# A mixer layer on one core: the first two row blocks modulated as a pair, x first in the queue, and even chunks

## The chip, the cores and the metric

The kernel runs on one core of a Trainium2 chip. The metric is the device time of one execution in microseconds, as the median of several runs. The engines are TensorE (PE; its weight loads are PEld), VectorE (DVE), ScalarE (ACT), GpSimd (POOL) and SyncE (SP, here only a queue that issues transfers).

## The reference

One layer of a decoder trunk on x of 512 x 2048, in float32:

```python
cond = jax.nn.silu(c)
mod = cond @ w_ada[l] + b_ada[l]
shift, scale, gate = jnp.split(mod, 3, axis=-1)
h = rms_norm(x, norm_g[l]) * (1.0 + scale[:, None, :]) + shift[:, None, :]
z = h @ w_in[l]
u_a, v_a, g_a, q_b, k_b, v_b, g_b, f_b = jnp.split(z, pts, axis=-1)
...
y = jnp.concatenate([y_a, y_b], axis=-1) @ w_out[l]
x = x + gate[:, None, :] * y
return rms_norm(x, final_g)
```

`y_a` is a chunked gated MLP of u, v and a gate, `y_b` is attention over 16 heads with a forget gate, times a gate. `c` is one vector of 2048, `w_ada` is 2048 x 6144 (shift, scale, gate), `w_in` 2048 x 7184, `w_out` 2048 x 2048.

## The kernel before

All big products are made of float32 operands cut into a high and a low part: three matmuls (high x high, high x low, low x high) for one. x and h are held transposed, as 16 row blocks of 128 model columns by 512 positions. A block k of h is made by `make_h` out of the transposed, normalised x (`xT[k]`) with a shift `sh` and a scale `gs` of one column each: `hh[k]` is its high, `hl[k]` its low part.

Shift and scale come from a product of one vector with w_ada. `ada_step(q, i)` loads a piece of w_ada (shift and scale columns of group q, some row blocks), and VectorE multiplies each row block by its element of silu(c), held as columns in `sc`, and adds it to an accumulator. `make_h(q)` then sums the accumulator over the partitions with matmuls of one column against `ones` (tile `mod`), adds the biases (L272 to L274) and makes hh and hl. The table `ADA` lists the groups: blocks 0 and 1 alone (pieces of 128 columns, four row blocks a load), all others in pairs (256 columns, two row blocks a load). Accumulators of the pairs and `mod` share the single PSUM bank with the tag "c".

At the start c, norm_g, b_ada and two small vectors are loaded to `rows` and turned into columns by TensorE; then x comes in four tiles of 128 positions, all on SP's queue. ScalarE squares each x tile (L311), the reciprocal root is taken (L91), VectorE scales the tile (L313), TensorE transposes it in pieces (L321) and ScalarE copies them out of PSUM (L325). Between these stand 32 matmuls on w_ada pieces that compute nothing that is used (`warm`, L208).

Then the first stage ("stream", tiles named `s` and `st`) multiplies 14 column groups of w_in (u and most of the gate of group A) with h, in chunks of row blocks listed in `CH`: six chunks of two and one of four. The 14 groups are in two sets, which share the same seven PSUM banks ("mm" four, "b" three): within a chunk one set runs, its partial sums are put aside or added (`sp`, L407 and L410), then the other set, which goes on in the next chunk. Each weight tile is loaded (`raw_st`), its high part made by ScalarE (L127) and its low part by VectorE or GpSimd (L128). During chunk q the steps of `ADA` for the blocks of chunk q+1 are put between the weight tiles; as many as fit into the tiles but one. `load` chains the transfers of SP's queue in the order of the program until the second chunk.

After the stream come value, query, key and gate groups of attention (`v_group`, `qk_group`, `g_group`), each with its banks from "mm"; a list of `fillers`, one taken after each weight tile, loads the gate columns of w_ada, which GpSimd sums, and `gate_sum` adds them over the partitions with a matmul. Attention slots, the rest of group A and the output projection follow. Instructions are ordered on each engine at build time by a planner that goes by priorities (`tc.high_priority`, `tc.issue_after`) and its own estimate of times.

Of the kernel before, what the change touches and what calls it, by code (L numbers as in the profile page):

```python
# [27 lines left out]
def trunk_kernel(  # L28
# [66 lines left out]
    CHAIN = [1]  # L95

# [59 lines left out]
    def col_group(segs, evs, name):  # L156
        nb = sum(w for _, w in segs) // P
        banks = [bank("mm", f"{name}_{b}") for b in range(nb)]
# [13 lines left out]
    rows = st.tile([80, P], F32, name="rows")  # L172
    nc.sync.dma_start(rows[0:16, :], c[0].rearrange("(a b) -> a b", b=P))
    nc.sync.dma_start(rows[16:32, :], norm_g[0].rearrange("(a b) -> a b", b=P))
    nc.sync.dma_start(rows[32:64, :], b_ada[0, 0 : 2 * D].rearrange("(a b) -> a b", b=P))
    nc.sync.dma_start(rows[64:72, :], ln_g[0].rearrange("(a b) -> a b", b=P))
    nc.sync.dma_start(rows[72:80, :], ln_b[0].rearrange("(a b) -> a b", b=P))

# [6 lines left out]
    cols_p = bank("c", "cols_p")  # L185
    nc.tensor.transpose(cols_p[:, 0:80], rows, ident[0:80, 0:80])
    cols = const.tile([P, 80], F32, name="cols")
    nc.vector.tensor_copy(cols, cols_p[:, 0:80])
# [13 lines left out]
    SPL = (0, 1)  # L202
    WARM = 4
    wbank = bank("c", "warm")

    def warm(src, n):
        for i in range(n):
            nc.tensor.matmul(wbank[:, 0:128], ident, src, start=True, stop=True)  # L208

    ADA = [(0, 1), (1, 1), (2, 2), (4, 2), (6, 2), (8, 2), (10, 2), (12, 2), (14, 2)]  # L210
    LANE = "DEDE"

    def ada_step(q, i):
        k0, nk = ADA[q]
        w = nk * P
        per = 4 // nk
        ga = st.tile([P, per, 2, w], F32, name=f"ada{q}_{i}", tag="ada", bufs=8)
        for s in range(2):
            load(
                ga[:, :, s, :], ada_r[:, i * per : (i + 1) * per, s, k0 * P : k0 * P + w]  # L220
            )
        if q == 0:
            warm(ga[:, 0, 1, :], WARM)
        if q in SPL:
            if i == 0:
                three = st.tile([P, 2, 256], F32, name=f"acca{q}", tag="acc", bufs=2)
                accs[q] = {
                    "D": three[:, 0, :].rearrange("p (s n) -> p s n", s=2),
                    "E": three[:, 1, :].rearrange("p (s n) -> p s n", s=2),
                }  # L230
            for j in range(per):
                kk = i * per + j
                ln = LANE[j]
                a = accs[q][ln]
                eng = nc.vector
                if i == 0 and ln not in LANE[:j]:
                    eng.tensor_scalar(a, ga[:, j], sc[:, kk : kk + 1], None, ALU.mult)
                else:
                    eng.scalar_tensor_tensor(a, ga[:, j], sc[:, kk : kk + 1], a, ALU.mult, ALU.add)
            return  # L240
        if i == 0:
            accs[q] = (
                bank("c", f"acc{q}"), st.tile([P, 2, 256], F32, name=f"accs{q}", tag="acc", bufs=2)
            )
        pt = accs[q][0]
        a = pt[:, 0 : 2 * w].rearrange("p (s n) -> p s n", s=2)
        sb = accs[q][1][:, :, 0:w]
        for j in range(per):
            kk = i * per + j
            if kk == 0:  # L250
# [633 lines left out]
```

## Time and profile before

| | us |
|---|---|
| median of 3 runs | 934.62 (934.34 to 935.93) |
| profiled execution | 936.01 |
| its span, first to last instruction | 934.3 |
| TensorE busy in it | 899.5 |

Times in the rows are microseconds from the start of the span. A row of a timeline gives the start, the duration, engine, line, operation, output and inputs with their shape, the count of instructions merged into it, and in square brackets the idle time of the engine ahead of it with what ended that. Shapes are partitions x elements. A window row gives for each engine the busy time and instructions in that stretch, then TensorE's granted clock as a share of 2.4 GHz, the busy share of the transfer engines and what they moved in GB/s.

### The profile page before, as it was taken

The page shows a single profiled execution, that of the slowest core. Times are in us where ns is not written, and L with a number is a line of the kernel's source. Part 1 is how long each engine was busy: PE and PEld are TensorE (multiplying, and loading weights), DVE is VectorE, ACT ScalarE, POOL GpSimd, SP SyncE. Part 2 cuts the span into 40 slices and gives each one's busy share as a digit, 9 for nine tenths or more (in the row PEclk, how much of TensorE's full clock was granted, in tenths as well). Part 3 has the DMA queues.
Part 4 walks back from the last instruction along what each step waited for, and adds up shares of the span by engine and source line. Part 5 has one row for each costly group of instructions (what it writes and reads, how often), then busy time and mean ns, then how long its engine had stood idle before and what let it go on. Part 6 is the DMA issues. An engine that isn't in the chain of part 4 may idle for free.

```text
span 934.3 us, 12387 instructions
## 1 busy us (share of the span) xinstructions
PE 899.5 (96%) x4485; PEld 764.7 (82%) x4485; DVE 537.0 (57%) x906; ACT 412.0 (44%) x724; POOL 325.5 (35%) x234
## 2 busy tenths in 40 slices
PE   4889989999999999999999999999999999999996
PEld 3768878889888887998889888998888888888884
DVE  4777776654545468456737664456424893445522
ACT  4634332353446446556436644556423532333311
POOL 1135553534002697897889910000000230000000
PEclk9999989999999999999999999999999999999999
DMA  8999997225333455435455443223233333446122
GB/s 297 333 356 351 305 300 231 80 61 140 100 92 113 120 171 152 158 117 168 143 163 180 148 114 99 82 70 91 77 103 90 102 106 116 151 143 226 61 111 91
DMA packets 117918, 142.75 MB, mean 153 GB/s; under 512 B 8400, under 2 KB 89504, under 8 KB 117344
## 3 DMA queue, kind: packets, MB, share of 16 engines
q1 hardware_dynamic: 117568, 141.43, 48.5%
q8 instruction: 35, 0.57, 0.3%
q10 hardware_dynamic: 288, 0.52, 0.2%
q14 instruction: 27, 0.22, 0.1%
HBM read 137.54 MB, written 4.19 MB: 152 GB/s over the span
## 4 chain that ended last, share of the span: by engine, by line
PE 86%; issue 2%; DMA 1%; DVE 1%; ACT 1%; POOL 1%; SPq 0%; POOLq 0%; ACTq 0%; DVEq 0%
PE s L143 5%; PE s L145 5%; PE s L144 5%; PE wo L154 5%; PE wo L153 5%; PE wo L152 5%; PE vb L153 3%; PE vb L154 3%; PE vb L152 3%; PE va L153 3%; PE k L143 3%; PE va L154 3%; PE va L152 3%; PE k L144 3%; PE k L145 3%; PE gb L144 3%
## 5 line engine op out<-in xcount | busy, mean ns | idle before, releaser
L603 POOL TENSOR_SCALAR gate<-gate,sc 128x512 f32<-128x512 f32 x60 | 108.6, 1818 | 21.5 <-DMA gate<-in_w_ada_dram 20.0
L143 PE MATMUL s<-hh,whi_st 128*128 128x512 f32 x224 | 87.5, 408 | 6.8 <-ACT hh L278 6.7
L128 POOL TENSOR_TENSOR wlo_st<-raw_st,whi_st 128x1024 fp32r<-128x1024 f32 (+3 forms) x32 | 63.8, 1999 | 82.8 <-ACT whi_st L127 81.3
L144 PE MATMUL s<-hl,whi_st 128*128 128x512 f32 x224 | 88.7, 396 | 2.3 <-POOL hl L289 2.3
L604 POOL TENSOR_TENSOR gate<-gate,gate 128x512 f32<-128x512 f32 x60 | 88.2, 1470 | 2.4
L145 PE MATMUL s<-hh,wlo_st 128*128 128x512 f32 x224 | 78.6, 396 | 0.0
L253 DVE SCALAR_TENSOR_TENSOR acc<-ada,sc,acc 128x512 f32<-128x512 f32 x98 | 74.0, 755 | 3.1
L152 PE MATMUL wo<-whi_wo,yh 128*128 128x512 f32 x192 | 74.8, 390 | 0.0
L153 PE MATMUL wo<-whi_wo,yl 128*128 128x512 f32 x192 | 74.7, 389 | 0.0
L153 PE MATMUL vb<-whi_vb,hl 128*128 128x256 f32 (+1 forms) x256 | 71.8, 286 | 0.0
L152 PE MATMUL vb<-whi_vb,hh 128*128 128x256 f32 (+1 forms) x256 | 71.8, 286 | 0.0
L154 PE MATMUL wo<-wlo_wo,yh 128*128 128x512 f32 x192 | 70.1, 390 | 0.0
L154 PE MATMUL vb<-wlo_vb,hh 128*128 128x256 f32 (+1 forms) x256 | 68.0, 285 | 0.0
L127 ACT ACTIVATE whi_st<-raw_st 128x1024 fp32r<-128x1024 f32 (+3 forms) x36 | 31.4, 873 | 80.5 <-PE s L144 44.4
L91 POOL TENSOR_TENSOR rsv<-rsv,nhalf 128x1 f32<-128x1 f32 x4 | 4.6, 1149 | 165.4 <-DVE rsv L90 165.4
L143 PEld LDWEIGHTS s<-hh,whi_st 128*128 128x128 f32 x224 | 43.5, 196 | 16.5 <-ACT hh L278 7.0
L849 POOL TENSOR_TENSOR sfin<-sfin,nhalf 128x1 f32<-128x1 f32 x4 | 2.2, 548 | 152.3 <-DVE sfin L846 152.3
L144 PEld LDWEIGHTS s<-hl,whi_st 128*128 128x128 f32 x224 | 42.9, 191 | 12.2 <-POOL hl L289 3.2
L143 PE MATMUL q<-hh,whi_q 128*128 128x512 f32 x128 | 50.4, 393 | 1.6 <-ACT ft L663 1.6
L143 PE MATMUL k<-hh,whi_k 128*128 128x512 f32 x128 | 50.4, 394 | 0.7 <-DVE q L455 0.7
L144 PE MATMUL gb<-hl,whi_gb 128*128 128x512 f32 x128 | 50.4, 394 | 0.0
L144 PE MATMUL q<-hl,whi_q 128*128 128x512 f32 x128 | 50.2, 393 | 0.0
(221 smaller groups left out, 2374.0 us busy)
## 6 DMA issues: line engine op xcount, KB each, us to landing
ada<-in_w_ada_dram SPq DMA_DIRECT2D x128, 256.0 KB
gate<-in_w_ada_dram SPq DMA_DIRECT2D x32, 512.0 KB
raw_wo<-in_w_out_dram SPq DMA_DIRECT2D x24, 512.0 KB
raw_q<-in_w_in_dram SPq DMA_DIRECT2D x16, 512.0 KB
raw_k<-in_w_in_dram SPq DMA_DIRECT2D x16, 512.0 KB
raw_gb<-in_w_in_dram SPq DMA_DIRECT2D x16, 512.0 KB
raw_va<-in_w_in_dram SPq DMA_DIRECT2D x16, 512.0 KB
raw_st<-in_w_in_dram SPq DMA_DIRECT2D x21, 384.0 KB
```

The costliest lines, as they stand in the source:

```text
L91: nc.gpsimd.tensor_tensor(dst, dst, nhalf[:, 0:1], ALU.pow)
L127: nc.scalar.activation(hi, raw, AF.Copy)
L128: (loeng or nc.vector).tensor_tensor(lo, raw, hi.bitcast(F32), ALU.subtract)
L143: nc.tensor.matmul(pt, hi[:, j, cs], hh[k], start=(k == first), stop=False)
L144: nc.tensor.matmul(pt, hi[:, j, cs], hl[k], start=False, stop=False)
L145: nc.tensor.matmul(pt, lo[:, j, cs], hh[k], start=False, stop=(k == last))
L152: nc.tensor.matmul(o, ah[k][:, tsl], hi[:, j, :], start=(k == first), stop=False)
L153: nc.tensor.matmul(o, al[k][:, tsl], hi[:, j, :], start=False, stop=False)
L154: nc.tensor.matmul(o, ah[k][:, tsl], lo[:, j, :], start=False, stop=(k == last))
L253: nc.vector.scalar_tensor_tensor(sb if kk == KB - 1 else a, ga[:, j], sc[:, kk : kk + 1], a, ALU.mult, ALU.add,)
L603: nc.gpsimd.tensor_scalar(ga[:, j], ga[:, j], sc[:, kk : kk + 1], None, ALU.mult)
L604: nc.gpsimd.tensor_tensor(a, a, ga[:, j], ALU.add)
```

## The change

Seven edits, most of them in the first stage.

- The small vectors are loaded on ScalarE's queue, c into a tile of its own; x is the first on SP's queue. c and the others are transposed apart, c into bank `cb`.
- 18 bf16 matmuls on a mask that is in SBUF from the start are put at TensorE's beginning (`BUSY`), and the 32 on w_ada pieces are dropped.
- `ADA` has pairs only: blocks 0 and 1 are modulated together, from eight steps of two row blocks with pieces of 256 columns. For this pair five of the 16 row blocks (`MV`) are multiplied on TensorE, as matmuls of one column into `cb`, to which the matmuls against `ones` then add.
- Block 0's h goes through a tile of its own on VectorE; block 1's hl is made by GpSimd as the others' are. The low part of the first weight tiles is made by GpSimd too.
- The x transposes 0 to 12 come ahead of the first `make_h`, and only the copies out of PSUM of 13 to 15 wait for its first activation; other banks are used for some.
- `CH` has eight chunks of two.
- The first query group takes its banks from the tags "b" and "c", and each `gate_sum` but the last comes three fillers later, the last after three empty ones.

```diff
-    rows = st.tile([80, P], F32, name="rows")
-    nc.sync.dma_start(rows[0:16, :], c[0].rearrange("(a b) -> a b", b=P))
...
+    crow = st.tile([16, P], F32, name="crow")
+    nc.scalar.dma_start(crow, c[0].rearrange("(a b) -> a b", b=P))
+    rows = st.tile([64, P], F32, name="rows")
+    for r0, nr, src in (
+        (16, 32, b_ada[0, 0 : 2 * D]), (0, 16, norm_g[0]), (48, 8, ln_g[0]), (56, 8, ln_b[0]),
+    ):
+        nc.scalar.dma_start(rows[r0 : r0 + nr, :], src.rearrange("(a b) -> a b", b=P))
...
+    cb = bank("c", "cb")
...
+    warm(cmask[:, 0:P], cmask[:, 0 : S - P], BUSY, True)
...
-    ADA = [(0, 1), (1, 1), (2, 2), (4, 2), (6, 2), (8, 2), (10, 2), (12, 2), (14, 2)]
-    LANE = "DEDE"
+    ADA = [(k, 2) for k in range(0, KB, 2)]
+    MV = (7, 9, 11, 13, 15)
...
+            if q == 0 and kk in MV:
+                for s in range(2):
+                    for n in range(2):
+                        newest_mm[0] = nc.tensor.matmul(
+                            cb[:, 2 * s + n : 2 * s + n + 1], ga[:, j, s, n * P : (n + 1) * P], col,
+                            start=(kk == MV[0] and s + n == 0), stop=False, skip_group_check=True,
+                        )
...
-            if q == 0:
+            h = xT[k]
+            if k == 0:
+                first_h[0] = z
+                h = st.tile([P, S], F32, name="h0", tag="acc", bufs=2)
                 nc.vector.tensor_scalar(
-                    xT[k], xT[k], gs[:, k : k + 1], sh[:, k : k + 1], ALU.mult, ALU.add
+                    h, xT[k], gs[:, k : k + 1], sh[:, k : k + 1], ALU.mult, ALU.add
                 )
...
-            (nc.vector if q == 0 else HL).tensor_tensor(hl[k], xT[k], hh[k].bitcast(F32), ALU.subtract)
+            (nc.vector if k == 0 else HL).tensor_tensor(hl[k], h, hh[k].bitcast(F32), ALU.subtract)
...
-    CH = [(0, 2), (2, 2), (4, 2), (6, 2), (8, 4), (12, 2), (14, 2)]
-    for i in range(4):
-        ada_step(0, i)
+    CH = [(0, 2), (2, 2), (4, 2), (6, 2), (8, 2), (10, 2), (12, 2), (14, 2)]
+    with tc.high_priority(offset=200):
+        for i in range(8):
+            ada_step(0, i)
...
-    HB = 8
+    HB = 12
...
-                        loeng=nc.gpsimd if gi in POOLG and (q or kk) else None,
+                        loeng=nc.gpsimd if gi in POOLG else None,
...
-                    if early:
-                        if gi:
-                            for f in early:
-                                f()
-                            early = []
+                    if q == 0 and kk == 0 and gi == 0:
                         continue
...
-        col_group([(Q0 + c0, 256)], [evac_q(2 * u), evac_q(2 * u + 1)], f"q{u}")
+        col_group([(Q0 + c0, 256)], [evac_q(2 * u), evac_q(2 * u + 1)], f"q{u}", "mm" if u else "x")
...
-                fillers.append(lambda g=g: gate_sum(g))
+                    if g and i == 2:
+                        fillers.append(lambda g=g: gate_sum(g - 1))
+            fillers.extend([lambda: None] * 3 + [lambda: gate_sum(3)])
```

## Rows read from the trace of the kernel before

**Rows 1.** The page's first part: busy time of each engine, its share of the span and its instructions.
```profile
PE 899.5 (96%) x4485; PEld 764.7 (82%) x4485; DVE 537.0 (57%) x906; ACT 412.0 (44%) x724; POOL 325.5 (35%) x234
```

**Rows 2.** Windows: from 240 us to the end, and the last of the windows of 20 us.
```profile
240.00:934.00 694.00, 684.57 (x3425) 581.87 (x3423) 380.69 (x642) 314.71 (x580) 228.93 (x153) 1.00 0.39 122
...
920.00:940.00 20.00, 5.27 (x24) 4.02 (x22) 2.69 (x5) 2.06 (x4) 0.55 (x1) 0.85 0.23 88
```

**Rows 3.** What TensorE's matmuls waited for over the whole span: us in total, times, longest.
```profile
PE s L143 <- ACT hh L278: 6.7, 3, 2.7
...
PE s L144 <- POOL hl L289: 2.3, 2, 2.0
PE q L143 <- ACT ft L663: 1.6, 1, 1.6
...
PE k L143 <- DVE q L455: 0.7, 1, 0.7
```

**Rows 4.** TensorE's timeline: transposes of x early and late in the ramp, the first matmul on hh, block 1, blocks 2 and 3, and the end of the stream.
```profile
11.98 1.75 PE L321 MATMUL xTp<-ident,x 128*128 128x128 f32 x7 [7.41 <-DVE x L313]
...
22.98 0.93 PE L321 MATMUL xTp<-ident,x 128*128 128x128 f32 x7
...
32.42 1.46 PE L143 MATMUL s<-hh,whi_st 128*128 128x512 f32 x5
...
37.59 0.72 PE L267 MATMUL mod<-ones,acca 128*128 128x1 f32 x6
39.82 1.91 PE L143 MATMUL s<-hh,whi_st 128*128 128x512 f32 x7 [1.51 <-ACT hh L278]
42.04 0.51 PE L144 MATMUL s<-hl,whi_st 128*128 128x512 f32 x1 [0.31 <-POOL hl L289]
...
58.30 1.88 PE L143 MATMUL s<-hh,whi_st 128*128 128x512 f32 x7 [2.47 <-ACT hh L278]
...
62.20 0.50 PE L144 MATMUL s<-hl,whi_st 128*128 128x512 f32 x1 [2.03 <-POOL hl L289]
...
207.53 0.28 PE L152 MATMUL vb<-whi_vb,hh 128*128 128x272 f32 x1
```

**Rows 5.** Groups of instructions by line and shape from 0 to 210 us: busy us, mean ns of one, idle time ahead of them. One of the stream's three kinds of matmul, the multiplies by silu(c), the added partial sums, and the low parts of weight tiles on GpSimd.
```profile
L143 PE MATMUL s<-hh,whi_st 128*128 128x512 f32 x224 | 87.5, 408 | 6.8 <-ACT hh L278 6.7
...
L253 DVE SCALAR_TENSOR_TENSOR acc<-ada,sc,acc 128x512 f32<-128x512 f32 x98 | 74.0, 755 | 3.1
...
L410 DVE TENSOR_TENSOR sp<-s,sp 128x512 f32<-128x512 f32 x42 | 28.3, 687 | 20.3 <-PE s L145 20.2
...
L128 POOL TENSOR_TENSOR wlo_st<-raw_st,whi_st 128x512 fp32r<-128x512 f32 x2 | 2.6, 1280 | 25.0 <-ACT whi_st L127 25.0
```

**Rows 6.** The chain that ended last, in order of time: start, us, what.
```profile
131.07 0.45 PE s L145 x2
...
132.21 0.80 PE mod L267 x8
...
135.71 0.79 PE s L143
```

**Rows 7.** Windows of 5 us with a granted clock under 1.00 (the value ahead of the transfer share).
```profile
60.00:65.00 5.00, 2.97 (x10) 2.25 (x10) 4.75 (x8) 0.36 (x1) 3.40 (x3) 0.83 1.08 361
65.00:70.00 5.00, 5.00 (x20) 4.06 (x19) 3.68 (x5) 0.63 (x2) 0.00 (x0) 0.83 1.09 354
...
135.00:140.00 5.00, 4.29 (x10) 3.38 (x11) 4.79 (x7) 2.77 (x4) 2.52 (x2) 0.50 0.85 262
140.00:145.00 5.00, 5.00 (x19) 4.00 (x19) 3.25 (x5) 0.00 (x0) 0.00 (x0) 0.82 0.96 322
```

**Rows 8.** Timelines of the ramp: SP's issues, ScalarE's pass over the last x tile, a weight pass and the copies, GpSimd's root and VectorE's scaling for the last x tile.
```profile
0.79 0.40 SPq L173 DMA_DIRECT2D rows<-in_c_dram  x1
...
2.89 2.08 SPq L104 DMA_DIRECT2D x<-in_x_dram  x4
...
15.27 1.91 ACT L311 ACTIVATE junk<-x 128x2048 bf16<-128x2048 f32 x1 [0.54 <-DMA x<-in_x_dram]
...
18.33 0.72 POOL L91 TENSOR_TENSOR rstd<-rstd,nhalf 128x1 f32<-128x1 f32 x1 [2.79 <-DVE rstd L90]
...
19.77 1.28 DVE L313 TENSOR_SCALAR x<-x,rstd 128x2048 f32<-128x2048 f32 x1
...
24.64 0.53 ACT L127 ACTIVATE whi_st<-raw_st 128x384 fp32r<-128x384 f32 x1
25.05 4.99 ACT L325 ACTIVATE xT<-xTp 128x512 f32<-128x512 f32 x10
```

**Rows 9.** Windows: while blocks 0 and 1 loaded w_ada, and two stretches in which pairs did. The last value is GB/s.
```profile
18.00:25.00 7.00, 7.00 (x47) 7.00 (x46) 6.67 (x16) 1.85 (x4) 0.72 (x1) 1.00 1.15 306
...
40.00:50.00 10.00, 9.69 (x42) 7.66 (x43) 9.26 (x14) 6.06 (x12) 2.59 (x2) 1.00 1.09 349
...
75.00:95.00 20.00, 20.00 (x93) 16.66 (x92) 17.37 (x28) 6.76 (x8) 12.16 (x7) 1.00 1.09 351
```

**Rows 10.** Timelines of GpSimd and VectorE around block 1: GpSimd's first low parts, and VectorE's wait for block 1's modulation and the first multiply for blocks 2 and 3.
```profile
37.64 2.23 POOL L128 TENSOR_TENSOR wlo_st<-raw_st,whi_st 128x512 fp32r<-128x512 f32 x2 [18.58 <-ACT whi_st L127]
...
38.35 0.16 DVE L272 TENSOR_TENSOR sh<-mod,cols 128x1 f32<-128x1 f32 x1 [4.49 <-PE mod L267]
...
38.84 0.74 DVE L251 TENSOR_SCALAR acc<-ada,sc 128x512 f32<-128x512 f32 x1
```

More of the change, by code (lines that the diff above doesn't have):

```diff
@@ L95, in trunk_kernel @@
     CHAIN = [1]
+    BUSY = 18
+    WARM = 0
     newest = [None]
@@ L154, in mm_toks, with col_group @@
                 nc.tensor.matmul(o, ah[k][:, tsl], lo[:, j, :], start=False, stop=(k == last))
-    def col_group(segs, evs, name):
+    def col_group(segs, evs, name, tag="mm"):
         nb = sum(w for _, w in segs) // P
-        banks = [bank("mm", f"{name}_{b}") for b in range(nb)]
+        banks = [bank(tag, f"{name}_{b}") for b in range(nb)]
         nk = 8 // nb
@@ L183, in trunk_kernel, with warm @@
         xt.append(xx)
-    cols_p = bank("c", "cols_p")
-    nc.tensor.transpose(cols_p[:, 0:80], rows, ident[0:80, 0:80])
-    cols = const.tile([P, 80], F32, name="cols")
-    nc.vector.tensor_copy(cols, cols_p[:, 0:80])
+    cb = bank("c", "cb")
+    def warm(lhs, rhs, n, first=False):
+        for i in range(n):
+            nc.tensor.matmul(
+                cb[:, P : P + rhs.shape[-1]], lhs, rhs, start=first, stop=True, skip_group_check=True
+            )
+    warm(cmask[:, 0:P], cmask[:, 0 : S - P], BUSY, True)
+    cols = const.tile([P, 80], F32, name="cols")
+    nc.tensor.transpose(cb[:, 16:32], crow, ident[0:16, 0:16])
+    nc.vector.tensor_copy(cols[:, 0:16], cb[:, 16:32])
+    cols_p = bank("b", "cols_p")
+    nc.tensor.transpose(cols_p[:, 0:64], rows, ident[0:64, 0:64])
+    nc.vector.tensor_copy(cols[:, 16:80], cols_p[:, 0:64])
     cT, ngT, bshT, bscT, lngb = (cols[:, 16 * i : 16 * (i + 1)] for i in range(5))
@@ L201, in trunk_kernel @@
     gate = gp_.tile([P, 4, 512], F32, name="gate")
[L202 to L208, printed above, removed]
-    ADA = [(0, 1), (1, 1), (2, 2), (4, 2), (6, 2), (8, 2), (10, 2), (12, 2), (14, 2)]
-    LANE = "DEDE"
+    ADA = [(k, 2) for k in range(0, KB, 2)]
+    MV = (7, 9, 11, 13, 15)
     def ada_step(q, i):
[L214 to L217, printed above, removed]
+        k0 = ADA[q][0]
+        ga = st.tile([P, 2, 2, 256], F32, name=f"ada{q}_{i}", tag="ada", bufs=8)
@@ L218, in ada_step @@
         for s in range(2):
-            load(
-                ga[:, :, s, :], ada_r[:, i * per : (i + 1) * per, s, k0 * P : k0 * P + w]
-            )
-        if q == 0:
[L223 to L240, printed above, removed]
@@ L241, in ada_step @@
-        if i == 0:
[L242 to L250, printed above, removed]
-                nc.vector.tensor_scalar(a, ga[:, j], sc[:, kk : kk + 1], None, ALU.mult)
+            load(ga[:, :, s, :], ada_r[:, 2 * i : 2 * i + 2, s, k0 * P : k0 * P + 256])
@@ new lines, in ada_step @@
+        if i == 0:
+            sb = st.tile([P, 2, 256], F32, name=f"accs{q}", tag="acc", bufs=2)
+            a = bank("c", f"acc{q}").rearrange("p (s n) -> p s n", s=2) if q else sb
+            accs[q] = (a, sb)
+        a, sb = accs[q]
+        for j in range(2):
+            kk = 2 * i + j
+            col = sc[:, kk : kk + 1]
+            if q == 0 and kk in MV:
[4 more added lines that the diff above has]
+                            start=(kk == MV[0] and s + n == 0), stop=False, skip_group_check=True,
+                        )
+            elif kk == 0:
+                nc.vector.tensor_scalar(a, ga[:, j], col, None, ALU.mult)
@@ L264, in make_h @@
         for s in range(2):
             for j in range(nk):
-                for n, part in enumerate(parts):
-                    newest_mm[0] = nc.tensor.matmul(
-                        mp[:, s * nk + j : s * nk + j + 1], part[:, s, j * P : (j + 1) * P],
-                        ones[:, 0:1], start=(n == 0), stop=(n == len(parts) - 1),
-                    )
+                newest_mm[0] = nc.tensor.matmul(
+                    mp[:, s * nk + j : s * nk + j + 1], accs[q][1][:, s, j * P : (j + 1) * P],
+                    ones[:, 0:1], start=q > 0, stop=True, skip_group_check=True,
+                )
@@ L369, in trunk_kernel @@
         ]
-        early = [f for z, (ka, _) in enumerate(ADA) if q == 0 and 0 < ka < sum(CH[0]) for f in ada_steps(z)]
         order = [0, 1] if (q + NQ) % 2 else [1, 0]
```

32 lines of the change are left out of this document (14 added, 18 removed).

## The prediction

> **What bounds the kernel now.** I read the profile from the whole to the place. The page's first part has TensorE at 96% of the span [rows 1]. The windows say where the rest is: from 240 us on it is idle for 9.4 us of 694, and 8.7 of these lie in the tail after 920 [rows 2]. So the change can only pay ahead of 240 us, where TensorE's waits and the granted clock tell what for. The waits name four causes behind the ramp: hh from ScalarE 6.7 us, hl from GpSimd 2.3, one wait of the first query group 1.6, and later one of 0.7 [rows 3].
>
> The first stretch is a ramp, then a stream. The stream begins with the first matmul on hh, at 32.42, and ends where the first value-group matmul starts, at 207.53 [rows 4]: 175.1 us. Its own work is 224 matmuls of each of three kinds (16 blocks x 14 column groups), 672 in all [rows 5]; two of them take 0.45 us in the chain, so one takes 0.2265 and all of them 152.2 us [rows 6]. Eight modulation matmuls take 0.80 [rows 6]; seven pairs of row blocks make 5.6 us, and block 1 some 1.0 us. The remainder is 175.1 - 152.2 - 6.6 = **16.3 us lost**. TensorE's timeline shows where [rows 4]: 1.51 us before block 1's hh and 0.31 before its hl; 2.47 and 2.03 us before blocks 2 and 3; and 2.7 us between the modulation of blocks 10 and 11 (132.21 + 0.80) and the matmul at 135.71 [rows 6]: 9.0 in all. The clock adds to it: in 60 to 70 us two windows of 5 us with mean 0.83 make 3.4 us at half rate (1.2 instead of 2.4 GHz), in 135 to 145 there are 6.8 us, 6.4 of them with work [rows 7]. Half of it is lost: 1.7 + 3.2 us. That leaves 2.4 us of restarts and small change.
>
> **The change part by part.**
>
> *x first.* SP issues five small loads from 0.79 us and x only at 2.89 [rows 8]; they go to ScalarE's queue, where five issues of 0.4 us end near 3 us, before the first x can have landed. x lands 2.1 us sooner: the last tile, which ScalarE starts at 15.27 [rows 8], at about 13.2.
>
> *Blocks 0 and 1 as a pair.* Both blocks' w_ada columns (16 loads of 256 KB, 4.19 MB) must now be there before the first matmul; before it was half. Against that the pieces grow from 512 B to 1 KB a row. With the short pieces the queue moved 306 GB/s, with the pairs' long ones 349 to 351 [rows 9]. 4.19 MB / 0.350 = 12.0 us, so the last lands at 13.2 + 12.0 = 25.2. The first two weight tiles (0.46 MB) follow by 26.5. VectorE multiplies 11 of 16 blocks instead of 16, each 0.755 us [rows 5], in all 8.3 us, and follows the loads: from tile 3 on it has one block per 1.5 us. TensorE takes the other five, 20 matmuls of one column; the nearest rows are six modulation matmuls in 0.72 us [rows 4], so 2.4 us, or 5 at half rate, among loads that they wait for anyway. After the last load: 0.3 us to start, 0.75 for VectorE, 0.5 for four modulation matmuls, and 1.5 from these to the matmul on hh (38.31 to 39.82 before [rows 4]). **Earliest start: 28.3.**
>
> The other chain is x. From ScalarE's last pass over x at 15.27 to the end of its scaling (19.77 + 1.28) it was 5.8 us [rows 8], so now about 19.0; then 13 copies out of PSUM at 0.5 us (ten in 4.99) and two weight passes of 0.6 [rows 8]: 26.7, just inside. If five of these copies stand behind the last load on ScalarE, or TensorE does the last 24 transposes after it, the start goes to 31 or 32. I take **29.3**, nearer to the lower end because both chains end there, 3.1 us before 32.42. The first lo parts move to GpSimd (1.28 us each [rows 5]): GpSimd had been idle for 18.6 us there [rows 10], it is needed only by the third matmul on, and costs nothing unless hl of block 1 queues behind it.
>
> *No wait at block 1.* Its 1.8 us go, and so does the delay that followed from it: VectorE sat 4.49 us until block 1's modulation matmuls, queued behind block 0's on TensorE, had run, and started on blocks 2 and 3 only at 38.84 [rows 10]. Now it starts at about 27.5. What is late next is w_ada of blocks 2 and 3: 4.19 MB plus 1.4 of the chunk's 1.84 MB of weights at 350 GB/s end at 25.2 + 16 = 41.2, VectorE at 42, and they are due when six of eight weight tiles are done, 29.3 + 14.3 = 43.6. The margin is small, so I keep one wait for hl as it stood there, 2.03 us, and its absence as the other end.
>
> *Chunks of two only.* A chunk takes 19.0 + 0.8 = 19.8 us of TensorE; it needs 6.03 MB, 17.2 us of transfers. VectorE has 16 x 0.755 and 7 partial sums added at 0.687 us [rows 5], 16.9 us. The one chunk of four had to prepare two pairs during the 20 us ahead of it; that is the stall at 133 us with its 6.8 us of slow clock. It goes: 2.7 + 3.2 = 5.9 us. The price is one more round of seven partial sums, 4.8 us of VectorE; the cover is the 2.9 us that VectorE has left in a chunk, and a stretch with just this load exists: 75 to 95 us, VectorE 17.4 and TensorE 20.0 of 20 us [rows 9].
>
> *First query group on other banks.* It waited 1.6 us for copies of the value group out of its banks [rows 3]. Value 1.6, other end 0 if the other banks or the weights are not ready either; the key group comes 21 us later and finds its banks free.
>
> *The gate sums* are put three steps later. No wait of TensorE for them is in rows 3; 0, and plus or minus 1 for the shifted turns of the banks. The 32 warming matmuls on w_ada fall away and 18 early ones come, in time in which TensorE has nothing else.
>
> **Sum.** Stream: 29.3 + 152.2 + 5.6 + lost time. Lost: 1.0 of restarts, 2.0 at block 2, 1.7 for one stretch of 3.4 us at half clock, since TensorE waits about 1.5 us ahead of the first matmul; 4.7 in all, with ends 0.5 and 8.5. End 191.8 against 207.5: 15.7, with the 1.6 of the query group **17.3 us**. The profiled execution took 936.01 us (span 934.3, and 1.7 around it that I leave); it would be 918.7. It lies 1.4 over the median of the runs, 934.62, which becomes **917.3**. Best case 28.3 and 0.5: 20.9 + 1.6 = 22.5, 912.1. Worst case 32 and 8.5: 9.2 + 0, 925.4.
>
> **The rivals.** *Cold start (0.17).* Seven transposes took 1.75 us at 11.98 and 0.93 at 22.98, after most of the warming matmuls on w_ada [rows 4]. So TensorE ran slowly in the gaps of the ramp and fast after steady work, though the granted clock reads 1.00 in both. The change has warming only in the first 8 us, ahead of those gaps. Then the 24 last transposes and the matvecs run at the slow rate and the stream starts at 31 with 6.8 us at half clock instead of 3.4: 1.7 + 1.7 us less gain, 920.7. The Trainium skill, "TensorE: Matmul & The Clock Gate", section on the clock gate, says that the low clock is the default and only sustained work lifts it; by that rule this speaks against the change, and the two rows of transposes agree with it. Against the rival: between 19 and 27 us transposes and matvecs themselves fill TensorE.
>
> *The start gains nothing (0.21).* In-order queues put x's scaling or the copies behind w_ada: start 32.4, block 2 keeps its waits and its clock (2.47 + 2.03 + 1.7) beside 2.3 of restarts. End 198.7, gain 8.8 + 1.6 = 10.4: 924.2. For it: x's last scaling already waited behind w_ada multiplies (its factor was ready at 19.05, it ran at 19.77 [rows 8]). Against it: x lands 2.1 us earlier and no warming matmul stands ahead of its transposes.
>
> *Slower (0.05): VectorE sets the pace of each chunk.* The multiplies of a pair start only after the pair before has been modulated, since both use one PSUM bank (38.84, right behind block 1's [rows 10]). 16.9 us of VectorE and 1.5 until hh are 18.4 of 19.8 us. If a chunk misses that, it pays as at 133 us, 5.9 us; three such chunks eat the gain, seven would give 917.3 + 41 = 958. Against it: 75 to 95 us.
>
> That the chunks do not even out, the stall at 133 staying while the rest works, I give 0.03: 917.3 + 5.9 = 923.2.
>
> **How the numbers follow.** The forecast has 0.54. Its own range, 912.1 to 922, and the rivals at 920.7, 923.2 and 924.2 lie within **912.5 to 925.0**, which leaves out the slower case and the two thin ends. A measurement here tells 0.2%, 1.9 us, from no change. Faster 0.94 (all but the slower rival and a little); the same 0.02; slower 0.04, as one or two such stalls would still leave it faster.
>
> **What would show it.** In the changed kernel: x passes on ScalarE from about 5.7; the last w_ada near 25; first hh matmul at 28.3 to 30; no gap at block 1; the first value-group matmul at 188 to 196; clock 1.00 from 45 to 240; no wait ahead of the first query group. Wrong: a start after 32, half clock in more than one stretch of the stream, or waits for hh at the chunk borders.

## The result, and the profile after

The changed kernel takes **921.17 us** (919.59 to 922.33), the kernel before in the same rounds 934.95 (934.34 to 935.93), four runs each: ratio 0.9851, with a 95% interval of 0.983 to 0.9871. That is 13.8 us faster; 917.3 was forecast, with a range of 912.5 to 925.0. The profiled execution took 922.11 us, its span is 920.4.

Line numbers have moved: the three matmul lines are now L145 to L147, x's transposes L313, the one-column matmuls on TensorE L237, the modulation L256, hh L267, the copies of the query group L445.

The first part of the profile's page, the answer to [rows 1]:

```profile
PE 898.9 (98%) x4504; PEld 763.0 (83%) x4504; DVE 528.7 (57%) x886; ACT 412.4 (45%) x724; POOL 326.4 (35%) x238
```

TensorE's busy time is the same within 0.6 us (899.5 before); what went is time in which it had no work. Its waits, as in [rows 3] (waiter, releaser: us in all, times, longest):

```profile
PE xTp L313 <- DVE x L306: 6.1, 2, 5.2
PE k L145 <- DVE q L445: 1.8, 1, 1.8
PE cb L191 <- POOL cmask L74: 1.5, 1, 1.5
PE s L145 <- ACT hh L267: 1.4, 1, 1.4
PE xTp L313 <- DVE rstd L90: 1.0, 1, 1.0
```

Of the waits of the stream only the first one for hh is left, 1.4 us. The wait for hl and that of the first query group are gone. A wait that was 0.7 is now 1.8: the second key group waits for copies of the second query group. TensorE's timeline, as in [rows 4]:

```profile
11.55 1.11 PE L313 MATMUL xTp<-ident,x 128*128 128x128 f32 x4 [5.19 <-DVE x L306]
...
26.10 1.07 PE L313 MATMUL xTp<-ident,x 128*128 128x128 f32 x8
27.00 0.95 PE L237 MATMUL cb<-sc,ada 128*128 128x1 f32 x8
27.82 1.09 PE L256 MATMUL cb<-ones,accs 128*128 128x1 f32 x8
30.33 2.50 PE L145 MATMUL s<-hh,whi_st 128*128 128x512 f32 x5 [1.42 <-ACT hh L267]
...
191.85 0.28 PE L154 MATMUL vb<-whi_vb,hh 128*128 128x272 f32 x1
...
216.05 0.40 PE L145 MATMUL q<-hh,whi_q 128*128 128x512 f32 x1
```

The stream starts at 30.33 and ends at 191.85; the forecast had 29.3 and 191.8. The first query matmul comes without a wait at 216.05, 17.5 us before that of the kernel before, whose row is:

```profile
233.53 0.50 PE L143 MATMUL q<-hh,whi_q 128*128 128x512 f32 x1 [1.64 <-ACT ft L663]
```

The span is only 13.9 shorter. So **3.6 us are given back behind 216 us.** The other engines in the ramp, the answer to [rows 8]: two rows of VectorE, four of ScalarE, the first of them an issue of its queue, and one of SP's queue:

```profile
18.77 6.26 DVE L244 SCALAR_TENSOR_TENSOR accs<-ada,sc,accs 128x512 f32<-128x512 f32 x8
25.65 0.75 DVE L244 SCALAR_TENSOR_TENSOR accs<-ada,sc,accs 128x512 f32<-128x512 f32 x1 [0.62 <-DMA ada<-in_w_ada_dram]
...
5.75 0.28 ACTq L180 DMA_DIRECT2D rows<-in_ln_v_b_dram  x1
6.05 1.28 ACT L304 ACT_TABLE_LOAD   x1 [6.05 <-DMA x<-in_x_dram]
7.35 1.91 ACT L304 ACTIVATE junk<-x 128x2048 bf16<-128x2048 f32 x1
...
13.56 1.91 ACT L304 ACTIVATE junk<-x 128x2048 bf16<-128x2048 f32 x1 [0.32 <-DMA x<-in_x_dram]
...
3.88 16.05 SPq L106 DMA_DIRECT2D ada<-in_w_ada_dram  x16
```

VectorE is through with the first pair at 26.40 (25.65 + 0.75); ahead of its last multiply it waited 0.62 us for the last load. TensorE starts the modulation only at 27.82, out of an unbroken run of transposes and matvecs: its own queue set the start. Windows (busy us and instructions of PE, PEld, DVE, ACT, POOL; TensorE's granted clock; busy share of the transfer engines; GB/s), as in [rows 7] and [rows 9]:

```profile
10.00:15.00 5.00, 2.46 (x10) 1.62 (x10) 3.46 (x6) 4.68 (x5) 1.27 (x3) 0.66 1.02 382
15.00:20.00 5.00, 4.11 (x25) 3.71 (x25) 4.49 (x9) 1.29 (x4) 1.05 (x1) 0.66 1.10 349
20.00:25.00 5.00, 5.00 (x50) 5.00 (x49) 4.79 (x7) 5.00 (x11) 0.00 (x0) 1.00 1.10 348
25.00:30.00 5.00, 3.91 (x36) 3.82 (x35) 1.34 (x6) 2.33 (x5) 2.22 (x2) 0.87 1.09 352
30.00:35.00 5.00, 4.67 (x11) 3.66 (x12) 4.89 (x8) 3.14 (x6) 1.28 (x1) 0.50 1.09 350
...
45.00:230.00 185.00, 185.00 (x932) 157.71 (x931) 125.60 (x201) 77.15 (x109) 88.97 (x64) 1.00 0.75 232
```

From 45 to 230 us TensorE is never without work and never below full clock. The start runs at half clock (0.50, 1.2 GHz) from about 28.7 to 35.5. And the place behind 216 us where time is given back: TensorE's timeline, then its windows of 1 us (busy, clock, DMA share, GB/s), and behind these the same place in the kernel before:

```profile
345.54 0.47 PE L145 MATMUL k<-hh,whi_k 128*128 128x512 f32 x1 [1.84 <-DVE q L445]
...
347.32 0.63 PE L147 MATMUL k<-hh,wlo_k 128*128 128x512 f32 x1
```

```profile
344.00:345.00 1.00, 0.00 (x0) 1.00 0.01 4
...
346.00:347.00 1.00, 1.00 (x5) 0.55 0.00 0
347.00:348.00 1.00, 1.00 (x4) 0.50 0.00 0
348.00:349.00 1.00, 1.00 (x3) 0.50 0.83 137
349.00:350.00 1.00, 1.00 (x5) 0.75 0.89 331
```

```profile
361.03 0.47 PE L143 MATMUL k<-hh,whi_k 128*128 128x512 f32 x1 [0.70 <-DVE q L455]
```

```profile
361.00:362.00 1.00, 0.97 (x4) 1.00 0.48 169
```

The wait is 1.1 us longer than before, and behind it some 3.4 us run at half clock, which loses 1.7; before, no window of 1 us from 360 to 365 was below 1.00. That is 2.8 of the 3.6; where the rest lies was not followed.

### The profile page after: what moved, and what is told of

The parts are those of the page before. It is cut to its first block, busy times and chain, and to the rows that moved or that the text cites. A ratio compares the mean times of both kernels' runs of the same rounds, so it can differ in the third digit from the quotient of the medians.

```text
span 920.4 us, 12414 instructions
## 1 busy us (share of the span) xinstructions
PE 898.9 (98%) x4504; PEld 763.0 (83%) x4504; DVE 528.7 (57%) x886; ACT 412.4 (45%) x724; POOL 326.4 (35%) x238
## 4 chain that ended last, share of the span: by engine, by line
PE 95%; DMA 2%; issue 1%; DVE 1%; ACT 0%; SPq 0%; POOLq 0%; POOL 0%; ACTq 0%; DVEq 0%
PE s L145 6%; PE s L147 6%; PE s L146 6%; PE wo L156 5%; PE wo L154 5%; PE wo L155 5%; PE vb L155 3%; PE vb L156 3%; PE vb L154 3%; PE k L145 3%; PE k L147 3%; PE gb L145 3%; PE gb L146 3%; PE k L146 3%; PE va L156 3%; PE gb L147 3%
## 5 line engine op out<-in xcount | busy, mean ns | idle before, releaser
L593 POOL TENSOR_SCALAR gate<-gate,sc 128x512 f32<-128x512 f32 x60 | 104.4, 1750 | 37.4 <-DMA gate<-in_w_ada_dram 34.5
L130 POOL TENSOR_TENSOR wlo_st<-raw_st,whi_st 128x1024 fp32r<-128x1024 f32 (+3 forms) x36 | 68.5, 1904 | 59.6 <-ACT whi_st L129 55.7
L145 PE MATMUL s<-hh,whi_st 128*128 128x512 f32 x224 | 88.0, 396 | 1.4 <-ACT hh L267 1.4
L147 PE MATMUL s<-hh,wlo_st 128*128 128x512 f32 x224 | 76.4, 395 | 0.0
L145 PE MATMUL k<-hh,whi_k 128*128 128x512 f32 x128 | 51.1, 399 | 1.8 <-DVE q L445 1.8
L145 PEld LDWEIGHTS s<-hh,whi_st 128*128 128x128 f32 x224 | 42.6, 191 | 10.1 <-ACT hh L267 1.5
L145 PE MATMUL q<-hh,whi_q 128*128 128x512 f32 x128 | 50.4, 394 | 0.0
L145 PE MATMUL gb<-hh,whi_gb 128*128 128x512 f32 x128 | 50.3, 393 | 0.0
```

The lines of the kernel that those rows point to most:

```text
L130: (loeng or nc.vector).tensor_tensor(lo, raw, hi.bitcast(F32), ALU.subtract)
L145: nc.tensor.matmul(pt, hi[:, j, cs], hh[k], start=(k == first), stop=False)
L147: nc.tensor.matmul(pt, lo[:, j, cs], hh[k], start=False, stop=(k == last))
L593: nc.gpsimd.tensor_scalar(ga[:, j], ga[:, j], sc[:, kk : kk + 1], None, ALU.mult)
```

## The experiments

Each of the groups e1 to e4, e5 to e8, e9 to e11 and e12 was timed beside runs of the kernel before, and the ratios are to those. "Start" and "end" are the first matmul on hh and the first value-group matmul of the profiled execution. One execution of each kernel was profiled. Edits are to the changed kernel unless a row says otherwise.

| | median us (range, runs) | ratio to before, 95% | start | end |
|---|---|---|---|---|
| the change | 921.17 (919.59 to 922.33, 4) | 0.9851 [0.983, 0.9871] | 30.33 | 191.85 |
| e1 query group on its old banks | 923.0 (921.26 to 929.27, 4) | 0.9886 [0.9851, 0.9921] | 31.09 | 192.06 |
| e2 gate sums as before | 921.23 (920.88 to 922.89, 4) | 0.9858 [0.9844, 0.9873] | 32.85 | 193.56 |
| e3 one chunk of four | 926.95 (924.89 to 927.09, 4) | 0.9909 [0.9893, 0.9926] | 32.88 | 198.55 |
| e4 TensorE kept busy | 922.07 (921.68 to 928.18, 4) | 0.9879 [0.9848, 0.991] | 33.78 | 193.45 |
| e5 no matvec on TensorE | 924.43 (923.82 to 927.55, 4) | 0.9898 [0.9874, 0.9921] | 34.62 | 195.63 |
| e6 no early matmuls | 921.76 (920.73 to 922.29, 4) | 0.9861 [0.9844, 0.9879] | 30.32 | 192.03 |
| e7 small loads first again | 924.76 (921.88 to 927.36, 4) | 0.9894 [0.9865, 0.9923] | 37.47 | 199.07 |
| e8 old banks, gap filled | 925.28 (922.94 to 932.59, 4) | 0.9892 [0.9866, 0.9918] | 41.19 | 202.25 |
| e9 before, even chunks alone | 929.55 (929.21 to 931.33, 4) | 0.9955 [0.9939, 0.9971] | 33.84 | 201.03 |
| e10 gate's tanh in place | 918.5 (917.56 to 918.76, 4) | 0.983 [0.9817, 0.9842] | 30.46 | 191.26 |
| e11 e10 with a filled ramp | 922.79 (922.44 to 931.06, 6) | 0.9906 [0.9873, 0.9938] | 35.36 | 196.56 |
| e12 e10 with three matvec blocks | 917.6 (917.42 to 918.43, 5) | 0.9815 [0.9796, 0.9834] | 30.71 | 191.45 |

**e1, the first query group on its old banks.**

```diff
-        col_group([(Q0 + c0, 256)], [evac_q(2 * u), evac_q(2 * u + 1)], f"q{u}", "mm" if u else "x")
+        col_group([(Q0 + c0, 256)], [evac_q(2 * u), evac_q(2 * u + 1)], f"q{u}")
```

> The changed kernel with one part undone: the first query group takes its banks from "mm" again. Its trace has the stream's end at 191.85 us, 15.7 before the old one, and the first query matmul at 216.05, 17.5 before; but the span only 13.9 shorter. 3.6 us are lost later, at a wait of 1.84 us ahead of the second key group and a stretch of 3.4 us at half clock behind it. Theory A: the other banks bring 1.6 to 1.8 us at the first query group and do not cause the later loss. Then the wait of about 1.6 comes back near 216, the later one stays: span 922.1. Theory B: the other banks shift the turns of the banks and the order of the attention work, and the later wait is their price. Then the early wait comes back and the late loss shrinks to the 0.7 of the kernel before: 920.4 + 1.7 - 2.8 = 919.3.

Its waits:

```profile
PE q L145 <- ACT ft L653: 1.6, 1, 1.6
...
PE k L145 <- DVE q L445: 0.8, 1, 0.8
```

The 1.6 of [rows 3] are back and the key group's wait is 0.8 again. From the first query matmul to the end of the span it is 701.4 us (919.5 - 218.06), after the change 704.35, before the change 700.8. From the first value matmul to that query matmul it is 26.0, after the change 24.2. So in this pair of profiles the other banks win 1.8 us at the first group and lose 2.95 behind it, as theory B has it (its span 919.3, shown 919.5). The profiles of eleven kernels with the old `silu2` agree on the waits: before, e1, e8 and e9, with the old banks, have 1.6 at the query group and 0.6 to 0.8 at the key group; the change and e2 to e7 have none and 1.6 to 1.9. They do not all lose as much behind it: from the first query matmul to the end it is 700.7 to 702.6 us in the four (mean 701.4), 702.3 to 704.35 in the seven (mean 703.1). That gives back 1.7, about what the first group wins. The two longest of the seven, the change (704.35) and e6 (704.3), are those in which half clock follows the wait; in the other five it does not. In the times the edit cannot be seen; the intervals overlap.

**e2, gate sums as before.**

```diff
-                    if g and i == 2:
-                        fillers.append(lambda g=g: gate_sum(g - 1))
-            fillers.extend([lambda: None] * 3 + [lambda: gate_sum(3)])
+                fillers.append(lambda g=g: gate_sum(g))
```

> The changed kernel with the gate sums put where they were before, each right behind its eight steps. Theory B': the later gate sums, not the banks, moved the attention work and made the wait of 1.84 us ahead of the second key group, with its 3.4 us at half clock. Then the span falls to about 917.6. Theory A/B: they cost and bring nothing: 920.4 within 0.5, with the late wait where it is.

921.23 against 921.17: the place of the gate sums brings and costs nothing, and the key group's wait is still 1.9. The clock behind that wait did not fall, as TensorE's window from the first key matmul (348.17) on shows (busy, clock, DMA share, GB/s):

```profile
348.00:353.00 5.00, 4.83 (x22) 1.00 0.59 182
```

The start of this profile, 32.85, is 2.5 us later than that of the change, though nothing in the ramp was edited; half clock lay from 9.0 to 22.6 us in it, from 11.6 to 18.4 in the change.

**e3, one chunk of four again.**

```diff
-    CH = [(0, 2), (2, 2), (4, 2), (6, 2), (8, 2), (10, 2), (12, 2), (14, 2)]
+    CH = [(0, 2), (2, 2), (4, 2), (6, 2), (8, 4), (12, 2), (14, 2)]
```

> The changed kernel with the chunk of four row blocks again in place of two of two. Theory: two pairs have to be prepared during the 20 us ahead of that chunk; block 10 and 11 come late, TensorE waits about 2.7 us for hh near 115 to 120 us and then runs 6.8 us at half clock: 5.9 us more, span 926.3. Rival: with the first pair together the multiplies run ahead, the slack covers two pairs, no wait: 920.4 within 1.

The waits, and a window of 10 us (PE busy, clock, DMA share, GB/s):

```profile
PE s L145 <- ACT hh L267: 4.1, 2, 2.7
```

```profile
125.00:135.00 10.00, 7.29 (x25) 0.83 0.95 298
```

The stall and half clock are back at the same chunk, and the time is 5.8 us longer, near the forecast's price (5.9). The trace shows a smaller one: a wait of 2.7 and half of 3.4 us at half clock (mean 0.83 over 10 us), not of 6.8, 4.4 in all. This profile's start was late as e2's was (32.88); from the start to the end of the stream it took 165.7 us, e2 160.7.

**e4, TensorE kept busy.** Matmuls on the mask, which add zero, between the matvecs and behind the modulation.

```diff
+                warm(cmask[:, 0:P], cmask[:, 0 : S - P], 4)
...
+        if q == 0:
+            warm(cmask[:, 0:P], cmask[:, 0 : S - P], 10)
```

> The changed kernel with matmuls on the zero mask added at the end of the ramp: four after each row block that TensorE multiplies, ten behind the modulation matmuls of the first pair. Nothing of their output is used. In the changed kernel the granted clock is half from 28.7 to 35.5 us, 5.2 us of it in the stream, which costs 2.6. Theory: the one-column matmuls of 24.4 to 28.9 and the gap of 1.42 us let the clock fall, and work in that time keeps it up: no half clock ahead of the stream, span 920.4 - 2.6 = 917.8. Rival: the added matmuls (30 of 0.16 to 0.32 us) stand in TensorE's queue ahead of the transposes and the modulation and put the start from 30.3 to 31.5 or 33, so that as much is lost: 920 to 922. Second rival: the clock falls all the same.

The clock stays at 1.00 from 20 us on, and the stream takes 159.7 us instead of 161.5. But it starts 3.45 us later: the added matmuls stand in the queue that sets the start. Without the half clock the stream is 1.8 us shorter, where 2.6 were expected; this filling costs more.

**e5, no matvec on TensorE.**

```diff
-    MV = (7, 9, 11, 13, 15)
+    MV = ()
...
-                    ones[:, 0:1], start=q > 0, stop=True, skip_group_check=True,
+                    ones[:, 0:1], start=True, stop=True, skip_group_check=True,
```

> The changed kernel with all 16 row blocks of the first pair multiplied on VectorE, none on TensorE. In the changed kernel VectorE ends its eleven at 26.4 us, but TensorE is through its transposes and one-column matmuls only at 27.9, so its queue sets the start of the stream. Theory: five more multiplies of 0.755 us put VectorE's end to about 29.5, and the first hh matmul from 30.3 to about 32; 1.5 to 2 us more, span about 922. Rival: TensorE's 20 one-column matmuls (0.12 us each, 2.4 in all) delayed the start as much as they spared, and they let the clock fall at 28.7; without them the start stays at 30 to 31 and the half-clock stretch in the stream is shorter: 918 to 920.

```profile
PE cb L256 <- DVE accs L244: 4.8, 1, 4.8
```

With all 16 blocks VectorE is the late one and TensorE waits 4.8 us for it. The five blocks on TensorE are worth 3 to 4 us.

**e6, no early matmuls.**

```diff
-    BUSY = 18
+    BUSY = 0
```

> The changed kernel without the 18 early matmuls on the mask. In the profiles so far the ramp's half-clock stretch lay at 11.6 to 18.5 us (start of the stream at 30.3) or at 9.2 to 22.8 (start at 32.9), with the early matmuls in all of them. Theory: they end at 6.2, nothing of TensorE follows until 11.5, so the clock falls again before the transposes and they bring nothing: start and span as in the changed kernel, 918 to 921. Rival: without them the clock stays low from the first transposes until some 23 us in each run, the start is always near 32.9: 921 to 923.

The stream starts at 30.32 instead of 30.33, and half clock lies ahead of and in the stream as it did (29.0 to 35.8, 28.7 to 35.5 in the change). The 18 early matmuls end at 6.2 us, 5.2 before the next long work, and bring nothing.

**e7, small loads first on SP's queue.**

```diff
-    crow = ...  nc.scalar.dma_start(crow, ...)
+    crow = ...  nc.sync.dma_start(crow, ...)
-        nc.scalar.dma_start(rows[r0 : r0 + nr, :], ...)
+        nc.sync.dma_start(rows[r0 : r0 + nr, :], ...)
```

> The changed kernel with the five small loads back on SP's queue, ahead of x. Theory: x, and w_ada behind it, come 2.1 us later, both chains of the ramp with them, and the stream starts 2 us later: first hh matmul near 32.5, span 922.5. Rival: TensorE's own queue of transposes sets the start and x has slack: 920.4 within 0.5.

Windows of 10 us (PE busy, clock, DMA share, GB/s):

```profile
10.00:20.00 10.00, 5.26 (x21) 0.50 1.03 380
20.00:30.00 10.00, 9.73 (x48) 0.50 1.10 350
30.00:40.00 10.00, 10.00 (x43) 0.50 1.09 354
```

In this execution the whole ramp ran at half clock, and the start came at 37.47. The kernel's four times go from 921.88 to 927.36, the fastest within the change's range. VectorE's last multiply of the first pair ends at 28.45 instead of 26.40, so x's place put this chain back by the 2.05 us that the theory had. The start came 7.1 us later, and how much of the loss of time is x's place and how much the clock is unsettled.

**e8, old banks and the gap behind the modulation filled** (the edit of e1 and the second one of e4).

> The changed kernel with the first query group on the old banks (as in e1, which ran the part behind the query group as fast as the kernel before) and ten matmuls on the zero mask behind the modulation matmuls of the first pair, in the gap of 1.42 us ahead of the stream; nothing of their output is used. Theory: the clock has fallen at 28.7 for what went before, but with the gap filled it rises after 3.4 us, at 32.1, instead of at 35.5: 1.7 us less than e1's 919.5, so 917.8. Rival: the ten matmuls at half rate take 3.2 us and stand ahead of the first hh matmul, the start moves by 1.5 and nothing is won: 919 to 921.

The theory fell. The profiled execution, 932.59 us, ran at half clock from 10 to 44 us, with the stream ending at 202.25; the other three took 922.94 to 926.57. Filling the gap did not pay in any of them; what it costs by itself this profile cannot tell, as the ramp ahead of it ran at half clock.

**e9, even chunks alone in the kernel before.** The edit of e3, the other way round.

> The kernel before with one part of the change alone: chunks of two row blocks only. e3, which undid this part in the changed kernel, was some 5.8 us slower than it. Theory: the part is independent of the rest: the wait of 2.7 us at 133 and its 6.8 us of half clock go here too, the waits at block 1 and at blocks 2 and 3 stay; 5.9 us less, 929 us. Rival: without the pair in front the multiplies lag behind, and the wait only moves to another chunk border: 932 to 935.

929.55 against 934.21: 4.7 us from this edit alone, against 5.8 in e3 the other way round. In the profile the stall at 133 us and its half clock are gone and the stream is 7.9 us shorter (167.2 instead of 175.1), but it starts 1.4 later. The waits for hh at block 1 and at blocks 2 and 3 stay (4.1 in two); that for hl at block 2, 2.03 before, is gone here too, without the pair.

**e10, the gate's tanh in place.** The question was why the key group waits at all. While the second query group runs, the banks of the second gate group are still unread: its tanh needs a tile `th`, and there are two of them, shared with the attention slots; while both are taken these banks cannot be read, and the key group is left with the banks that the query group has to leave first. The tanh is now written where the result goes.

```diff
-        th = pool.tile([P, S], F32, name=f"th_{name}", tag="th", bufs=2)
+        th = dst
```

> The changed kernel with one edit in the gate of group B: its tanh goes into the tile of the result instead of a tile with the tag "th", which has two buffers and is shared with the attention's tm tiles. In the changed kernel the two banks of the second gate group are read only at 354 us, long after its last matmul near 313, so that the second key group has to take the banks of the query group before it and waits 1.84 us for their copies. Theory: the shared tile held the gate's banks; now they are read near 315, the key group finds free banks, the wait of 1.84 and the 3.4 us of half clock behind it go, and what the other banks for the first query group brought is kept: 920.4 - 1.8 - 1.7 = 916.9 span, 918 as a median. Rival: the banks are free, but ScalarE's and VectorE's order is moved and a wait of like size stands elsewhere: 919 to 922.

The reading of the gate's last two banks, first in the changed kernel, with the last matmuls into them, then in e10 (by tile `gb` from 290 or 310 us: engine, operation, count, durations in ns, first and last start):

```profile
L147 PE MATMUL gb<-hh,wlo_gb x3: 387/390/397, 310.3 to 312.8; 128*128 128x512 f32 x3
...
L345 ACT ACTIVATE th_b<-gb x2: 599/600/602, 354.2 to 355.6; 128x512 f32<-128x512 f32 x2
```

```profile
L345 ACT ACTIVATE sgB<-gb x2: 597/599/601, 307.6 to 327.3; 128x512 f32<-128x512 f32 x2
```

In the changed kernel they are held for 41 us after the last matmul and read after the second key group has begun (345.54). In e10 they are free before it, and its wait is gone. The kernel before held them nearly as long, 39 us: its last matmul into them starts at 330.4, and they are read from 369.5:

```profile
L350 ACT ACTIVATE th_b<-gb x2: 598/600/602, 369.5 to 371.0; 128x512 f32<-128x512 f32 x2
```

So the held banks are why the key group waits at all; the other banks of the first query group are why it waits 1.84 and not 0.7. TensorE's timeline of e10 at its first matmul, with no idle time ahead of it:

```profile
342.15 0.39 PE L145 MATMUL k<-hh,whi_k 128*128 128x512 f32 x1
```

From the first query matmul to the end it is now 700.3 us (915.8 - 215.47), 4.0 less than after the change; e11 and e12, which have this edit too, have 700.2. The median of 918.5 us lies below both kernels'; the slowest run (918.76) lies below the change's fastest (919.59), as do e12's five, though they were timed on other chips than the change, and the intervals against before overlap.

**e11, e10 with a filled ramp.** 28 matmuls on the mask behind the transpose of c, four behind each of the first three scaled x tiles (`WARM` 0 to 4), and four `sgB` tiles.

> e10 with a fourth tile for the gate, 28 more matmuls on the zero mask behind the early 18, and four matmuls behind each of the first three scaled x tiles; nothing of their output is used. Theory: the ramp's half-clock stretches differ from run to run (11.6 to 18.5 in one profile, 9.2 to 22.8 or 10.1 to 40.9 in others), because TensorE is thinly used from 6 to 19 us; with that filled the clock is up from some 6 us on in each run, the first hh matmul is at 30.3 each time, and the runs lie closer: 0.5 to 1 us less than e10 as a median, 916.5 to 918, with a spread under 1.5. Rival: the added work stands in the queue ahead of the transposes and delays the start by 1 to 2 us: 919 to 921.

```profile
28.68 4.47 PE L191 MATMUL cb<-x,ident 128*128 128x128 f32 x24
32.99 0.95 PE L257 MATMUL cb<-ones,accs 128*128 128x1 f32 x8
35.36 2.07 PE L145 MATMUL s<-hh,whi_st 128*128 128x512 f32 x4 [1.42 <-ACT hh L268]
```

The planner put the twelve fillers on x tiles (24 instructions in the trace) right ahead of the modulation, and the start moved by 4.9 us against e10's 30.46, 4.47 of it theirs. The rival was right, by more than it had said, and the six runs lie no closer (922.44 to 931.06).

**e12, e10 with three matvec blocks.**

```diff
-    MV = (7, 9, 11, 13, 15)
+    MV = (11, 13, 15)
```

> The version with the gate group's tanh in place (918.5 us, its stream started at 30.46), with three instead of five row blocks of the first pair on TensorE (11, 13 and 15); VectorE takes 13. Theory: TensorE's own queue set the start, as it was through with matvecs and transposes only at 27.95 in the changed kernel while VectorE had ended at 26.40. Eight one-column matmuls fewer, of 0.11 us each (16 in 1.84), take 0.9 us from TensorE; VectorE gets two multiplies of 0.755 more, 1.5 us, part of them in its waits for the loads: it ends at 27.0 to 27.9. The modulation then starts near 27.2 instead of 27.8, the stream at about 29.8, and the time is 917.9, hardly to be told from 918.5. Rival 1: VectorE becomes the late one, as with no matvec at all (start 34.62, of which 4.8 were its waits): start at 31.5 or later, with a wait of TensorE for accs above 1 us, and 920 to 922. Rival 2: the ramp's clock decides whatever the split is: the time is then explained by the half clock that the profile shows between 10 and 45 us, and not by the start of VectorE's last multiply.

TensorE's timeline, and VectorE's:

```profile
27.33 1.86 PE L256 MATMUL cb<-ones,accs 128*128 128x1 f32 x8 [0.20 <-DVE accs L244]
30.71 2.50 PE L145 MATMUL s<-hh,whi_st 128*128 128x512 f32 x5 [1.52 <-ACT hh L267]
...
18.65 8.62 DVE L244 SCALAR_TENSOR_TENSOR accs<-ada,sc,accs 128x512 f32<-128x512 f32 x11
```

VectorE ends at 27.27 and the modulation starts 0.06 us later, at 27.33 instead of e10's 28.01, so both queues now end together. But it ran at half clock (1.86 us for its eight instructions instead of 1.03), which took the 0.7 us back. 917.6 cannot be told from e10's 918.5.

## Why the prediction was right, and where it was off

The forecast was that TensorE is the bound, so that only what ends the stream earlier counts, and by how much. Its terms against the profiled execution after:

| step | forecast | shown |
|---|---|---|
| start of the stream | 29.3 | 30.33 |
| lost in it (restarts 1.0, hl 2.0, clock 1.7) | 4.7 | 3.7 (191.85 - 30.33 - 152.2 - 5.6) |
| end of the stream | 191.8 | 191.85 |
| first query group | 1.6 | 1.8, then given back |
| behind it | 0 | -3.6 |
| span | -17.3 | -13.9 |

*The start* was 1.0 late in this profile. Transfers were as foreseen: 348 to 352 GB/s, and VectorE finished with the last of them (26.40). The last x pass starts at 13.56, near the forecast's 13.2, after a wait of 0.32 for its tile. The first starts at 7.35 and not at 5.7: the five issues on ScalarE's queue do not end near 3 us, the fifth stands at 5.75 (why, no row shows), and an activation table load of 1.28 us, which the kernel before has at 0.79, comes behind it. What the forecast left as a bound, TensorE doing the late transposes and matvecs, became the limit: it was done at 27.82. The forecast had made this queue too short. It took 2.4 us for the 20 matvec matmuls and 0.5 for the four modulation matmuls, as if each were one instruction of the rows; the trace has two for each of them, 40 and 8 (x8 in 1.09 at 27.82), as it has 32 for the 16 warming matmuls in the program of the kernel before:

```profile
L237 PE MATMUL cb<-sc,ada 128*128 128x1 f32 x40 | 4.8, 238 | 0.0
```

e5 and e12 show both sides of the split: no matvec on TensorE is 4.3 us later, three blocks instead of five bring the modulation forward by 0.7. The ramp's clock moves the start as well: with the change's ramp unedited it came at 30.33, 31.09 (e1), 32.85 (e2), 32.88 (e3) and 30.46 (e10), and the two late ones are those with half clock to 22.6 us. So 30.33 is one outcome of at least two.

*The lost time* was made up differently. The wait for hl at block 2, which the forecast kept at 2.0 with its absence as the other end, did not come. The half clock took more: 5.2 us of it lie in the stream, 2.6 lost instead of 1.7. The two errors and the late start cancel, so the end of the stream is right by 0.05 us partly by luck.

*Even chunks* were priced at 5.9 and measured at 5.8 (e3) and 4.7 (e9); by e3's trace the stall itself was 4.4, as less half clock followed it than before. The cover that was named for the extra sums on VectorE held: no wait in 185 us. *The gate sums* were worth nothing, as said (e2).

*The pair* was not undone alone. The waits at block 1 (1.51 and 0.31) and at blocks 2 and 3 (2.47 and 2.03) are gone in the change, and e9 keeps three of the four; how the rest of the gain divides between the pair and x's place stays open.

*The step that failed* is the first query group. The wait was rightly read and its removal rightly sized at the place, but "the key group comes 21 us later and finds its banks free" looked only at the first key group. The second, 130 us on, had a wait of 0.7 in [rows 3]; it grew to 1.84, and in this profile half clock followed, together 2.8 of the 3.6 us given back. e10 shows what holds it: with the gate's banks read earlier the whole loss goes. That the other banks lengthened it from 0.7 is shown by the waits of eleven kernels (under e1); how each bank moves in between was not followed. Over these profiles the step is worth nothing (1.8 won, 1.7 given back) and not 1.6.

*The cold-start rival* (920.7, nearest to the result) was half right. The transposes at 11.55 did run at half rate, 0.28 us each, against 0.13 at 26.10, and half clock lay over the start. But the start was 30.33 and not 31, the half clock cost 2.6 us and not 3.4, and the median lies near 920.7 for another reason, the 3.6 us given back late. In e2 and e3 the start was even later than the rival's. *The start gains nothing* has its start (32.4) shown by e2 and e3, but not by the change; its price is refuted, as the waits at block 2 that it kept are gone (e2's stream ends at 193.56, not 198.7). *VectorE sets the pace* is refuted by 185.00 of 185 us.

## What to carry to other kernels

When one engine is 98% busy, follow a removed wait to the end of the program: the tiles or banks that it takes from others come back as a wait elsewhere, and the gain of the place (1.8 us here) says nothing of the whole. A short idle time on TensorE can cost about as much again in clock behind it (1.84 us, then 1.7), but need not: in five of seven kernels a wait of 1.6 to 1.9 at this place was followed by none. A ramp's start read from one profile is one outcome: unedited, it came at 30.33 and at 32.88. And look for what keeps a PSUM bank from being read: here two scratch tiles that others also use held two banks for 41 us, and writing in place brought the median down by 2.7 us.

## What the runs showed of the hardware

**The clock in the ramp differs from run to run and kernel to kernel, at nearly the same work.** Half clock lasted to 18.4 us in the change, to 22.6 in e2 with the same ramp, and through to 40.4 in e7 and 44.1 in e8, although TensorE was busy for 9.73 and 10.00 us of two windows of 10 there (e7's rows). e8's four times span 9.7 us. The Trainium skill, "TensorE: Matmul & The Clock Gate", Part 1, says that how many matmuls run slowly at the start differs between runs of the same kernel, and puts the ramp's penalty under 1% of a typical span; the ramps of the change and e2 agree with the first. Against the second stands that e8's slowest run took 9.65 us more than its fastest of 922.94, 1.05%; its stream started 10.1 us later than e1's, but the fastest run has no trace, so that the ramp makes all of the difference is not shown.

**The clock fell while TensorE was still at work.** In the change TensorE had no gap from 20 us to 28.9, the later part of it mostly matmuls of one column; 25 to 30 us has a mean clock of 0.87 and 30 to 35 of 0.50, so it was down from about 28.7, ahead of the gap and not behind it. With wide bf16 matmuls between the others (e4) it stayed at 1.00 from 20 to 50 us.

**The clock did not fall behind every wait of the same length.** Ahead of the second key group TensorE waited 1.84 us in the change and 1.7 in e6, and half clock followed; it waited 1.9, 1.7, 1.7, 1.6 and 1.6 in e2, e3, e4, e5 and e7, and the clock stayed at 1.00.

**The clock column can read 1.00 where TensorE ran at half rate.** In e6 it reads 1.00 up to 29.0 us, yet four transposes at 11.59 took 1.11 us, as at 11.55 in the change, where it reads 0.50 from 11.6 to 18.4; at 26.15 eight took 1.07. So the prediction's two rows of transposes, 0.25 and 0.13 us each at a clock of 1.00, are no contradiction: in the ramp the durations tell the rate, and the column may not.
